# Down projection of the gated MLP: 16 of 22 feature blocks by Strassen's seven products, operand sums on GpSimd

## The chip, the core and the metric

One core of one Trainium2 chip runs the whole program in one launch. The metric is device time in microseconds (us); the median of three runs is compared. Engines are named as in the profile: PE (TensorE), ACT (ScalarE), DVE (VectorE), POOL (GpSimd), SP (SyncE, which here issues nearly all DMAs).

## What is computed

An encoder of two layers, batch 1, 1024 tokens, model width 1024, everything in float32. Layer 0 mixes tokens by latent attention and retention, layer 1 by gated linear attention. Each layer ends with the same MLP, and only its last product is touched here:

```python
def _conv_ffn(x, norm_g, w_up, conv_w, conv_b, w_down):
    h = _rmsnorm(x, norm_g)
    up = h @ w_up                                  # (1024, 1024) @ (1024, 2 * 2816)
    gate, val = up[..., :D_FF], up[..., D_FF:]
    gate = lax.conv_general_dilated(gate, ...) + conv_b    # depthwise, width 3
    return (jax.nn.silu(gate) * val) @ w_down      # (1024, 2816) @ (2816, 1024)
...
        x = x + _conv_ffn(x, ffn_norm[layer], ...)
```

## The kernel before

Activations lie transposed: features on the 128 partitions, tokens along the free dimension. A feature block is 128 features, a half is 512 tokens. The 2816 hidden features are 22 blocks (`NF`), the model width is 8 blocks (`NK`). Every float32 operand is held as two float32r parts, high and low, made by `split` (L327 on ACT writes the high part, L328 on DVE the low part), and every product is three matmuls (`mm3`, L349: high by high, high by low, low by high), each of one 128x128 weight block by 512 tokens.

**Up stage.** `up_fast` makes hidden block i (gate and value, both halves) by Strassen's algorithm in Winograd's form: seven products of four `mm3` instead of eight, with sums of weights on DVE (L1222 to L1225) and sums of activations kept in pages h1 to h4 (`T`). `gated_mid` applies the convolution and the gate; the result `cv` (128x1024) goes to DRAM (L1273, tile d).

**Down stage.** `down` computes the second product plainly. For each half of the tokens it holds all 22 hidden blocks as high and low parts (hx for the first 8, gh for the other 14), read back from d through the staging pages st (L1287). For each output block m it loads the weights in three pieces of 8, 8 and 6 hidden blocks (`wtile`, L340, pages raw), splits them (pages w), runs 66 matmuls into one PSUM bank, and adds the residual x (L1343). So a down stage has 2 x 8 x 66 = 1056 matmuls of 512 columns. In layer 0 the result is also normed for the next layer (`norm_add` L386 and L388, `norm_parts` L407); in layer 1 it is transposed (L1306) and written out.

**Order.** The tile framework puts each engine's instructions in an order of its own from the program's text, its dependences and its own estimates; each engine then runs its list strictly in that order, and waits on semaphores. SP's DMA issues are such a list too. A page of a pool is reused when its last reader is done.

Of the kernel before, what the change touches and what calls it, by code (L numbers as in the profile page):

```python
# [66 lines left out]
class Encoder:  # L67
# [1208 lines left out]
    def down(self, layer, mid, xs, gain=None, ahead=None):  # L1276

        nc, io = self.nc, self.io
        wdn = io["ffn_w_down"][layer].rearrange("(k p) f -> p k f", p=P)
        parts = [{}, {}]  # L1280

        def load(hf, ks):
            for k in ks:
                if k % 2 == 0:
                    two = self.page([P, 2, H2], tag="st")
                t = two[:, k % 2]
                nc.sync.dma_start(out=t, in_=mid[k][:, halves()[hf]])  # L1287
# [262 lines left out]
```

## Time and profile before

| | us |
|---|---|
| median of 3 runs | 2576.71 (2576.38 to 2578.4) |
| the profiled execution, its own time | 2580.83 |
| its span in the profile | 2579.0 |
| PE busy in the span | 2535.9 (98%) |
| DVE / ACT / POOL busy | 1649.4 / 1182.5 / 148.4 |
| mean granted PE clock | 0.998 |

The profiled execution took 4.1 us more than the median; 1.8 us of its time lie outside the span. Busy times of engines overlap, so they don't add up. Matmuls are pipelined: a matmul of 512 columns is shown with about 390 ns, but such matmuls follow one another at a shorter distance.

### The profile page before, as it was taken

Reading aid. Unit: us, or ns where it says so; the run is one execution under the profiler, and the core shown is the slowest. Engines: PE = TensorE matmul, PEld = TensorE weight load, DVE = VectorE, ACT = ScalarE, POOL = GpSimd, SP = SyncE. Lnnn points to the kernel's source line nnn. Section 1 sums busy time; section 2 is a strip of 40 time slices with the busy share of each in tenths; the row PEclk is TensorE's granted clock in tenths of the full one; section 3 lists DMA queues with packets and bytes.
Section 4 is the critical chain, followed back from the end, with each engine's and each line's share of the span. In section 5 each row is a group of like instructions: output and inputs, shape, how many; then the busy total and the mean of one; then the engine's idle time right before and its main releaser. Section 6 shows DMA issues by size and latency. Waiting matters only on the chain.

```text
span 2579.0 us, 33115 instructions
## 1 busy us (share of the span) xinstructions
PE 2535.9 (98%) x12776; PEld 2125.0 (82%) x12776; DVE 1649.4 (64%) x2607; ACT 1182.5 (46%) x2155; POOL 148.4 (6%) x222
## 2 busy tenths in 40 slices
PE   8999999999999999999999999999999999999999
PEld 8989877777888888887888898897788888887887
DVE  6545887878578677776363545648588776775331
ACT  5234767778444333344242445657443333334221
POOL 0000033443000000000000000000000000000000
PEclk9999999999999999999999999999999999999999
DMA  5111100003622222238443111223732222237443
GB/s 194 40 46 42 50 26 5 14 18 123 212 83 81 82 82 87 85 110 275 141 146 95 58 54 46 75 65 122 242 97 69 84 82 82 82 116 254 142 140 92
DMA packets 320596, 253.81 MB, mean 98 GB/s; under 512 B 14828, under 2 KB 271957, under 8 KB 320437
## 3 DMA queue, kind: packets, MB, share of 16 engines
q1 hardware_dynamic: 317877, 243.30, 30.2%
q0 software_dynamic: 2560, 8.39, 0.8%
q8 instruction: 100, 1.64, 0.3%
q14 instruction: 59, 0.48, 0.1%
HBM read 193.71 MB, written 57.93 MB: 98 GB/s over the span
## 4 chain that ended last, share of the span: by engine, by line
PE 84%; DVE 6%; ACT 5%; DMA 2%; issue 2%; SPq 0%; POOL 0%; DVEq 0%; ACTq 0%
PE mm L349 74%; PE mr L1102 1%; ACT w L327 1%; PE mr L349 1%; PE mr L1389 1%; PE mr L1444 1%; PE mr L1391 1%; DMA st<-d 1%; PE mr L852 1%; PE mr L1032 1%; DMA raw<-in_w_out_odd 1%; PE mr L1077 1%; DVE w L328 1%; DVE hx L328 1%; DVE sr L1445 1%
## 5 line engine op out<-in xcount | busy, mean ns | idle before, releaser
L349 PE MATMUL mm<-hx,w 128*128 128x512 f32 (+1 forms) x3600 | 867.7, 393 | 1.6 <-ACT hx L1241 1.4
L349 PEld LDWEIGHTS mm<-hx,w 128*128 128x128 f32 (+1 forms) x3600 | 670.6, 188 | 144.8 <-ACT hx L1241 2.2
L328 DVE TENSOR_TENSOR w<-raw,w 128x1024 fp32r<-128x1024 f32 (+2 forms) x271 | 297.1, 1098 | 301.3 <-ACT w L327 284.0
L327 ACT CAST w<-raw 128x1024 fp32r<-128x1024 f32 (+2 forms) x321 | 285.3, 893 | 415.6 <-PE mm L349 358.0
L349 PE MATMUL mm<-w,hx 128*128 128x256 f32 (+1 forms) x2304 | 364.4, 306 | 2.3 <-POOL w L328 1.7
L349 PE MATMUL mm<-h,wf 128*128 128x512 f32 x1368 | 328.9, 389 | 0.0
L349 PEld LDWEIGHTS mm<-w,hx 128*128 128x128 f32 x2304 | 308.1, 192 | 21.5 <-POOL w L328 2.7
L349 PE MATMUL mm<-gh,w 128*128 128x512 f32 x1344 | 314.7, 392 | 4.5 <-ACT gh L327 3.6
L349 PEld LDWEIGHTS mm<-h,wf 128*128 128x128 f32 x1368 | 256.8, 188 | 53.3
L349 PEld LDWEIGHTS mm<-gh,w 128*128 128x128 f32 x1344 | 250.2, 188 | 61.2 <-ACT gh L327 5.3
L1239 DVE TENSOR_TENSOR hx<-mm,hx 128x512 f32<-128x512 f32 x190 | 130.4, 687 | 154.1 <-PE mm L349 154.0
L327 ACT CAST wf<-raw 128x1024 fp32r<-128x1024 f32 x78 | 81.9, 1053 | 187.6 <-DVE raw L1225 118.1
L349 PE MATMUL mm<-hx,wf 128*128 128x512 f32 x552 | 131.9, 389 | 0.0
L349 PEld LDWEIGHTS mm<-hx,wf 128*128 128x128 f32 x552 | 103.6, 188 | 21.5
L349 PE MATMUL mm<-h,w 128*128 128x512 f32 x456 | 109.5, 389 | 0.0
L349 PE MATMUL mm<-hr,hr 128*128 128x512 f32 x336 | 104.1, 404 | 1.3 <-ACT hf L1473 1.3
L328 DVE TENSOR_TENSOR wf<-raw,wf 128x1024 fp32r<-128x1024 f32 x78 | 95.1, 1221 | 12.5 <-ACT wf L327 12.4
L349 PEld LDWEIGHTS mm<-h,w 128*128 128x128 f32 x456 | 85.6, 188 | 17.7
L1269 ACT ACTIVATE pg<-pg 128x1024 f32<-128x1024 f32 x44 | 46.7, 1062 | 107.1 <-DVE pg L1268 106.9
L1268 DVE SCALAR_TENSOR_TENSOR pg<-mm,c,pg 128x512 f32<-128x512 f32 (+1 forms) x100 | 74.0, 747 | 33.0 <-ACT pg L1263 32.9
L349 PE MATMUL mm<-hf,w 128*128 128x512 f32 x384 | 88.8, 392 | 0.0
L349 PEld LDWEIGHTS mm<-hf,w 128*128 128x128 f32 x384 | 72.2, 188 | 16.0
(364 smaller groups left out, 3057.3 us busy)
## 6 DMA issues: line engine op xcount, KB each, us to landing
raw<-in_ffn_w_up SPq DMA_DIRECT2D x88, 512.0 KB
raw<-in_ffn_w_down SPq DMA_DIRECT2D x64, 512.0 KB
st<-d SPq DMA_DIRECT2D x95, 256.0 KB
d<-pg SPq DMA_DIRECT2D x44, 512.0 KB
raw<-in_ffn_w_down SPq DMA_DIRECT2D x32, 384.0 KB
raw<-in_w_in_odd SPq DMA_DIRECT2D x24, 512.0 KB
raw<-in_w_out_even SPq DMA_DIRECT2D x16, 512.0 KB
raw<-in_w_out_odd SPq DMA_DIRECT2D x16, 512.0 KB
```

What stands on the lines that cost most here:

```text
L327: self.nc.scalar.copy(hi, src)
L328: return (rest or self.nc.vector).tensor_tensor(lo, src, hi.bitcast(F32), ALU.subtract)
L349: mm = lambda w, x, start, stop: self.nc.tensor.matmul(out, lhsT=w, rhs=x, start=start, stop=stop, skip_group_check=more)
L852: self.nc.tensor.transpose(ps[:, blk(j)], src[:, j], self.ident)
L1032: nc.tensor.matmul(ps[:, n], lhsT=k3[:, t % 4], rhs=vt(t), start=True, stop=True)
L1077: nc.tensor.matmul(p[:, blk(j)], lhsT=kc[:, blk(j)], rhs=qc[:, blk(j)], start=True, stop=True)
L1102: nc.tensor.matmul(ps, lhsT=w[:, blk(t % 4)], rhs=x, start=n == 0, stop=n == len(terms) - 1)
L1239: add = lambda out, x, y: nc.vector.tensor_tensor(out, x, y, ALU.add)
L1268: nc.vector.scalar_tensor_tensor(dst, g[hf][:, src], cw(tap), dst, ALU.mult, ALU.add)
L1269: nc.scalar.activation(cv, cv, AF.Silu)
L1389: nc.tensor.matmul(ps[:, :192], lhsT=e.cq[k][hf][:, blk(t % 4)], rhs=w1[:, k], start=k == 0, stop=k == 2)
L1391: nc.tensor.matmul(ps[:, 256:], lhsT=e.ckv[k][hf][:, blk(t % 4)], rhs=w2[:, k], start=k == 0, stop=k == 1)
```

## The change

Hidden blocks 0 to 15 go through Strassen's algorithm in the down projection, in two windows (w = 0 and 1) of eight blocks; blocks 16 to 21 stay plain.

- In a window, the even hidden blocks are the upper and the odd ones the lower half of the inner dimension, the two halves of the tokens are the two column blocks, and output blocks m and m + 1 are the two row blocks. A *visit* is one window and one pair of output blocks: seven products of four `mm3`, 84 matmuls, where the plain way takes 96. There are 8 visits in a layer (four pairs, two windows).
- The four sums of hidden blocks that Strassen needs are made in the up stage by POOL (`Mid.add`, four subtractions for each pair of blocks), and written to DRAM behind the next weight loads (`flush`). The tile d becomes seven operands for each window, 4 x 256 KB each.
- `operands` reads one operand of a window back (two loads of 512 KB through the pages pg and st) and splits it. Window 0's are read during the last steps of the up stage, into pages h1 to h4 and hx as these come free; window 1's during visit 3, each right behind the product that was the last to use its place. `rest` reads blocks 16 to 21 during visit 7.
- The weights of a visit are loaded once for both halves (four loads of 256 KB); their four sums are made by POOL (`weights`, `part`), and each of the seven is split by ACT and DVE six products ahead (`LEAD`).
- Each product is added by DVE into the residual or into a helper u (the first of window 0 copied by ACT); PSUM banks b1, b3 and b4 are used by two products of a visit, and the second accumulates on the first. After visits of window 1 POOL adds u to three results.
- The stores of the residual in `out_proj` are issued by ACT instead of POOL, and the program's scratch for software DMA is set to 4096.

```diff
+PAIRED, WIN, LEAD = 16, 8, 6
...
                 if hf:
                     for j in range(2):
-                        nc.gpsimd.dma_start(out=xs[2 * m + j], in_=self.xT[m][j])
+                        nc.scalar.dma_start(out=xs[2 * m + j], in_=self.xT[m][j])
...
-        mid = []
-        with self.room("left", h2=8), self.room("left", h3=8), self.room("left", h1=8), self.room("left", h4=8):
-            T = {n: [tuple(self.page([P, H2], F32R, f"h{n}") for _ in range(2)) for _ in range(4)] for n in range(1, 5)}
+        mid = Mid(self)
+        with ExitStack() as stack:
+            for n in (2, 3, 1, 4):
+                h4 = stack.enter_context(self.room("left", **{f"h{n}": 4}))
+            T = {n: self.pairs(f"h{n}") for n in range(1, 5)}
             self.xrooms.pop().close()
+            late = stack.enter_context(self.room("left", tt=4))
...
+            down = Down(self, layer, mid)
...
-                for g, then in zip(steps, steps[1:] + [None]):
+                for i, (g, then) in enumerate(zip(steps, steps[1:] + [None]), 3):
                     next(g)
                     if then:
                         next(then)
+                    else:
+                        for p in range(1, 5):
+                            down.operands(0, p)
+                        down.begin()
                     for _ in g:
                         pass
-        if gain is not None:
-            self.x_rooms()
-            with self.room("left", st=2), self.room("left", gh=28):
-                return self.down(layer, mid, xs, gain, ahead)
-        with self.room("left", st=2), self.room("left", gh=28), self.room("right", xt=8, yt=2):
-            self.down(layer, mid, xs)
+                    if i == PAIRED:
+                        mid.flush()
+                        late.close()
+                        late = stack.enter_context(self.room("left", st=1, wd=2))
+                    if i == NF - 2:
+                        down.operands(0, 0)
+                for p in range(5, 7):
+                    down.operands(0, p)
+            return down.run(xs, gain, ahead, stack, (late, h4))
+    def pairs(self, tag):
+        pages = [[self.page([P, 2, H2], F32R, tag) for _ in range(2)] for _ in range(2)]
+        return [tuple(x[:, j % 2] for x in pages[j // 2]) for j in range(4)]
...
+        mid.flush()
...
-        d = self.dp.tile([P, S], F32, name=self.nm("d"))
-        nc.sync.dma_start(out=d, in_=cv)
-        mid.append(d)
...
+        mid.add(i, cv)
...
+class Mid:
...
+        self.d = [[[e.waiting() for _ in range(2)] for _ in range(7)] for _ in range(PAIRED // WIN)]
+    def add(self, i, cv):
+        e, nc = self.e, self.e.nc
+        if i >= PAIRED:
+            d = e.dp.tile([P, 2, H2], F32, name=e.nm("d"))
+            nc.sync.dma_start(out=d.rearrange("p h f -> p (h f)"), in_=cv)
+            self.last.append(d)
+            return
+        w, j = divmod(i // 2, WIN // 2)
+        at = lambda p: self.d[w][p][j // 2][j % 2]
+        two = [cv[:, sl] for sl in halves()]
+        if i % 2 == 0:
+            self.first = two
+            nc.sync.dma_start(out=at(0), in_=two[0])
+            return
+        b11, b12, b21, b22 = *self.first, *two
+        nc.sync.dma_start(out=at(2), in_=b21)
+        nc.sync.dma_start(out=at(6), in_=b22)
+        t1, t2, t3, t4 = (e.page([P, H2], tag="tt") for _ in range(4))
+        for t, x, y in ((t1, b12, b11), (t2, b22, t1), (t3, b22, b12), (t4, b21, t2)):
+            nc.gpsimd.tensor_tensor(t, x, y, ALU.subtract)
+        self.late += [(at(p), t) for p, t in ((4, t1), (1, t2), (3, t3), (5, t4))]
+    def flush(self):
+        for d, t in self.late:
+            self.e.nc.sync.dma_start(out=d, in_=t)
+        self.late = []
...
+class Down:
...
+    A11, S2, A12, S3, S1, A22, S4 = range(7)
...
+    def operands(self, w, p):
+        e, nc, n = self.e, self.nc, {1: 2, 3: 3, 4: 1, 5: 4}.get(p)
+        out = e.pairs(f"h{n}") if n else [tuple(e.page([P, H2], F32R, "hx") for _ in range(2)) for _ in range(4)]
+        self.b[w][p] = out
+        for a, d in enumerate(self.mid.d[w][p]):
+            self.n = getattr(self, "n", -1) + 1
+            two = e.page([P, 2, H2], tag="st" if self.n % 4 == 3 else "pg")
+            nc.sync.dma_start(out=two, in_=d.rearrange("j p f -> p j f"))
+            if n:
+                e.split(two, *(bass.AP(x.tensor, x.offset, [list(x.ap[0]), [H2, 2], [1, H2]]) for x in out[2 * a]))
+            else:
+                for j in range(2):
+                    e.split(two[:, j], *out[2 * a + j])
+    def weights(self, v):
+        e, nc, (w, m) = self.e, self.nc, self.visits[v]
+        wg, wv = (e.page([P, 2, WIN // 2, P], F32, "raw") for _ in range(2))
+        for x, c in ((wg, m), (wv, m + 1)):
+            src = self.w[:, blk(w, WIN), blk(c)].rearrange("p (j two) f -> p two j f", two=2)
+            for i in range(2):
+                nc.sync.dma_start(out=x[:, i], in_=src[:, i])
+        s1, s4 = (e.page([P, WIN // 2, P], tag="hx") for _ in range(2))
+        nc.gpsimd.tensor_tensor(s1, wv[:, 0], wv[:, 1], ALU.add)
+        nc.gpsimd.tensor_tensor(wv[:, 0], wg[:, 0], wv[:, 0], ALU.subtract)
+        self.raw[v] = {self.A11: wg[:, 0], self.S2: wg[:, 0], self.A12: wg[:, 1], self.S3: wv[:, 0], self.S1: s1,
+                       self.A22: wv[:, 1], self.S4: s4}
+    def part(self, s):
+        if s >= 7 * len(self.visits):
+            return
+        e, nc, (v, p) = self.e, self.nc, divmod(s, 7)
+        if not p:
+            self.weights(v)
+        r = self.raw[v]
+        t = e.page([P, 2, WIN // 2, P], F32R, "wd" if p in (self.S1, self.A22) else "w")
+        e.split(r[p], t[:, 0], t[:, 1])
+        self.parts[s] = t
+        if p == self.A11:
+            nc.gpsimd.tensor_tensor(r[p], r[self.S1], r[p], ALU.subtract)
+        if p == self.A12:
+            nc.gpsimd.tensor_tensor(r[self.S4], r[p], r[self.S2], ALU.subtract)
+    def begin(self):
+        for s in range(LEAD):
+            self.part(s)
+    def product(self, s, ps, first):
+        t, b = self.parts.pop(s), self.b[self.visits[s // 7][0]][s % 7]
+        for j in range(WIN // 2):
+            self.e.mm3(ps, (t[:, 0, j], t[:, 1, j]), b[j], first and j == 0, j == WIN // 2 - 1, not first)
+    def visit(self, v):
+        e, nc, (w, m) = self.e, self.nc, self.visits[v]
+        last = m == NK - 2
+        for i in range(2):
+            for hf in range(2):
+                if not w:
+                    nc.sync.dma_start(out=self.x[m + i][hf], in_=self.xs[2 * (m + i) + hf])
+        (c11, c12), (c21, c22) = self.x[m], self.x[m + 1]
+        if not w:
+            self.u[m] = e.page([P, H2], tag="hx")
+        u = self.u[m]
+        b1, b2, b3, b4 = (e.bank() for _ in range(4))
+        for p, (ps, outs) in enumerate(((b1, [u]), (b2, [u]), (b1, [c11]), (b3, [c22]), (b4, [c22]), (b3, [c21]), (b4, [c12]))):
+            s = 7 * v + p
+            self.product(s, ps, p in (0, 1, 3, 4))
+            for x in outs:
+                if not w and p == 0:
+                    nc.scalar.copy(x, ps)
+                else:
+                    nc.vector.tensor_tensor(x, ps, x, ALU.add)
+            self.part(s + LEAD)
+            if last and not w:
+                self.operands(1, p)
+            if last and w and p in (1, 3, 4):
+                self.rest({1: 0, 3: 2, 4: 4}[p], {1: 2, 3: 3, 4: 1}[p])
+        if w:
+            for x in (c21, c12, c22):
+                nc.gpsimd.tensor_tensor(x, x, u, ALU.add)
+    def rest(self, k, n):
+        e = self.e
+        for k in (k, k + 1):
+            two = e.page([P, 2, H2], tag="st" if k % 4 == 3 else "pg")
+            self.nc.sync.dma_start(out=two, in_=self.mid.last[k])
+            parts = [e.page([P, 2, H2], F32R, f"h{n}") for _ in range(2)]
+            e.split(two, *parts)
+            self.b[1][7 + k] = parts
...
+    def run(self, xs, gain, ahead, stack, ends):
+        e, nc, io = self.e, self.nc, self.e.io
+        self.xs, self.u = xs, {}
+        if gain is not None:
+            e.act_set(LN_EXP)
+            e.x_rooms()
+            e.new_x()
+            self.x = e.xT
+        else:
+            stack.enter_context(e.room("right", xt=2 * NK))
+            self.x = [[e.page([P, H2], tag="xt") for _ in range(2)] for _ in range(NK)]
+        for v in range(len(self.visits)):
+            self.visit(v)
+        if gain is None:
+            for room in ends:
+                room.close()
+            stack.enter_context(e.room("left", yt=2))
...
+        for hf in range(2):
+            for m in range(NK):
+                wh, wl = e.wtile(self.w[:, PAIRED:, blk(m)], [P, NF - PAIRED, P])
+                ps, x = e.bank(), self.x[m][hf]
+                for k in range(NF - PAIRED):
+                    b = [t[:, hf] for t in self.b[1][7 + k]]
+                    e.mm3(ps, (wh[:, k], wl[:, k]), b, k == 0, k == NF - PAIRED - 1)
...
+    nc = bacc.Bacc("TRN2", target_bir_lowering=False, num_devices=1, dynamic_dma_scratch_size=4096)
```

How instructions stand, at three places.

**ACT, start of layer 0's down stage.** Before: the casts of step 21's gate (pg) and of the hidden blocks (st) follow one another, and nothing that PE needs for a used PSUM bank stands among them.

```order
L1263 ACTIVATE pg_10743<-hx_10612,c_70 128x512
L327 CAST hx_10796<-st_10794 128x512
L327 CAST hx_10801<-st_10794 128x512
L1269 ACTIVATE pg_10743<-pg_10743 128x1024
L327 CAST hx_10807<-st_10805 128x512
L327 CAST hx_10812<-st_10805 128x512
L327 CAST gh_10818<-st_10816 128x512
L327 CAST gh_10823<-st_10816 128x512
L327 CAST w_10980<-raw_10978 128x1024
```

Now: from the gate of step 21 (pg_10956) through the casts of operands 5 (h) and 6 (hx) to the copy of the first product of visit 0, which is the last row.

```order
L1281 ACTIVATE pg_10956<-hx_10719,c_70 128x512
L328 CAST h_10968<-pg_10972 128x1024
L328 CAST h_10970<-st_10976 128x1024
L1287 ACTIVATE pg_10956<-pg_10956 128x1024
L328 CAST hx_10980<-pg_10988 128x512
L328 CAST hx_10982<-pg_10988 128x512
L328 CAST hx_10984<-pg_10994 128x512
L328 CAST hx_10986<-pg_10994 128x512
L145 ACT_TABLE_LOAD
L1415 COPY hx_11028<-mm_11029 128x512
```

The copy that clears bank mm_11029 for its second product stands behind both casts of operand 6's second load and an activation table load.

**DVE, middle of the down stage.** Before: output blocks 5 and 6 of the first half; between two evictions (L1343) stand three low parts of weights and one sum of squares.

```order
L1343 TENSOR_TENSOR xb_10904<-mm_11355,xb_10904 128x512
L328 TENSOR_TENSOR w_11552<-raw_11549,w_11551 128x768
L388 TENSOR_TENSOR pg_11082<-pg_11082 128x512
L328 TENSOR_TENSOR w_11581<-raw_11578,w_11580 128x1024
L328 TENSOR_TENSOR w_11611<-raw_11608,w_11610 128x1024
L1343 TENSOR_TENSOR xb_10906<-mm_11488,xb_10906 128x512
L328 TENSOR_TENSOR w_11641<-raw_11638,w_11640 128x768
L388 TENSOR_TENSOR pg_11082<-pg_11082 128x512
```

Now: visit 3, while window 1's operands come in (h and hx are operands, mm_11428 to mm_11431 are the visit's four banks b1 to b4, w are weights).

```order
L329 TENSOR_TENSOR h_11498<-pg_11503,h_11497 128x1024
L1417 TENSOR_TENSOR xb_11020<-mm_11428,xb_11020 128x512
L329 TENSOR_TENSOR w_11520<-raw_11481,w_11520 128x512
L329 TENSOR_TENSOR hx_11524<-pg_11531,hx_11523 128x512
L1417 TENSOR_TENSOR xa_11023<-mm_11430,xa_11023 128x512
L329 TENSOR_TENSOR hx_11526<-pg_11531,hx_11525 128x512
L329 TENSOR_TENSOR w_11556<-raw_11481,w_11556 128x512
L329 TENSOR_TENSOR hx_11528<-st_11537,hx_11527 128x512
L329 TENSOR_TENSOR h_11561<-pg_11564,h_11560 128x1024
L329 TENSOR_TENSOR hx_11530<-st_11537,hx_11529 128x512
L329 TENSOR_TENSOR h_11563<-pg_11568,h_11562 128x1024
L1417 TENSOR_TENSOR xa_11023<-mm_11431,xa_11023 128x512
```

Between the evictions of bank b3 (mm_11430) and bank b4 (mm_11431) stand six low parts, five of them of operands; all six are first needed in the next visit.

## Rows read from the trace of the kernel before

**Rows 1.** Page, part 1: busy us of each engine, share of the span, instructions.

```profile
PE 2535.9 (98%) x12776; PEld 2125.0 (82%) x12776; DVE 1649.4 (64%) x2607; ACT 1182.5 (46%) x2155; POOL 148.4 (6%) x222
```

**Rows 2.** Windows: from:to, length, busy us by engine, PEclk, DMA share, GB/s.

```profile
830.00:1143.00 313.00, 313.00 (x1383) 259.26 (x1382) 228.63 (x317) 110.57 (x132) 0.00 (x0) 1.00 0.26 83
1180.00:1200.00 20.00, 19.14 (x81) 14.58 (x81) 12.12 (x17) 10.83 (x17) 0.00 (x0) 1.00 0.91 288
1200.00:1410.00 210.00, 210.00 (x929) 173.92 (x928) 93.25 (x117) 70.90 (x95) 0.00 (x0) 1.00 0.49 150
2360.00:2574.00 214.00, 213.62 (x971) 176.56 (x969) 67.16 (x75) 56.84 (x74) 0.00 (x0) 1.00 0.46 138
```

**Rows 3.** Timeline, PE: start us, us, engine, line, operation, count.

```profile
1165.81 11.04 PE L349 MATMUL mm<-hx,w 128*128 128x512 f32 x48
...
1394.79 5.60 PE L349 MATMUL mm<-hx,w 128*128 128x512 f32 x24
...
1409.75 5.60 PE L349 MATMUL mm<-hx,w 128*128 128x512 f32 x24
...
2322.76 11.06 PE L349 MATMUL mm<-hx,w 128*128 128x512 f32 x48
...
2563.81 9.81 PE L349 MATMUL mm<-gh,w 128*128 128x512 f32 x42
```

**Rows 4.** Chain that ended last, longest pieces: start us, us, what.

```profile
1174.96 4.48 DMA st<-d
...
2339.29 5.33 DMA st<-d
...
2378.73 15.02 PE mm L349 x66
2394.18 15.00 PE mm L349 x66
```

**Rows 5.** Timeline, layer 1: a weight load issued, and the waiting cast.

```profile
2359.94 1.25 SPq L340 DMA_DIRECT2D raw<-in_ffn_w_down  x2
...
2364.26 1.06 ACT L327 CAST w<-raw 128x1024 fp32r<-128x1024 f32 x1 [3.56 <-DMA raw<-in_ffn_w_down]
```

**Rows 6.** Groups by line, DVE, 1166 to 1410 us: count, busy, mean ns.

```profile
L328 DVE TENSOR_TENSOR w<-raw,w 128x1024 fp32r<-128x1024 f32 x30 | 36.7, 1225 | 85.9 <-ACT w L327 85.6 <-DMA st<-d 0.3
L328 DVE TENSOR_TENSOR gh<-st,gh 128x512 fp32r<-128x512 f32 x28 | 18.5, 690 | 12.1 <-ACT gh L327 12.0
L328 DVE TENSOR_TENSOR w<-raw,w 128x768 fp32r<-128x768 f32 x16 | 15.3, 955 | 0.7 <-PE mm L349 0.6
L407 DVE SCALAR_TENSOR_TENSOR pg<-xb,c,pg 128x512 f32<-128x512 f32 x8 | 5.7, 748 | 0.1
L1343 DVE TENSOR_TENSOR xa<-mm,xa 128x512 f32<-128x512 f32 x8 | 5.5, 691 | 11.7 <-PE mm L349 11.7
```

**Rows 7.** Groups by line, ACT, same stretch.

```profile
L327 ACT CAST w<-raw 128x1024 fp32r<-128x1024 f32 x31 | 32.6, 1051 | 87.8 <-PE mm L349 80.2 <-issue 4.4 <-DMA raw<-in_ffn_w_down 3.2
L327 ACT CAST gh<-st 128x512 fp32r<-128x512 f32 x28 | 17.1, 621 | 16.3 <-DMA st<-d 15.7
```

**Rows 8.** Groups by line, POOL, whole span.

```profile
L328 POOL TENSOR_TENSOR w<-raw,w 128x512 fp32r<-128x512 f32 x48 | 63.8, 1329 | 125.8 <-ACT w L327 82.6 <-issue 15.5 <-PE mm L349 13.0
```

**Rows 9.** One line (L1501): count, shortest/median/longest ns.

```profile
L1501 DVE SCALAR_TENSOR_TENSOR pg<-pg,pg x8: 685/1623/1725, 441.1 to 656.4; 128x512 f32<-128x512 f32 x8
```

**Rows 10.** Timeline of DVE and POOL around one of those eight.

```profile
514.98 1.29 POOL L328 TENSOR_TENSOR w<-raw,w 128x512 fp32r<-128x512 f32 x1 [2.56 <-PE mm L349]
515.15 1.67 DVE L1501 SCALAR_TENSOR_TENSOR pg<-pg,pg 128x512 f32<-128x512 f32 x1
```

**Rows 11.** Timeline of DVE, one step of the up projection.

```profile
1098.47 1.29 DVE L1271 TENSOR_TENSOR pg<-pg,hx 128x512 f32<-128x512 f32 x2
...
1103.45 0.69 DVE L1239 TENSOR_TENSOR hx<-mm,hx 128x512 f32<-128x512 f32 x1 [0.55 <-PE mm L349]
...
1108.88 0.69 DVE L1239 TENSOR_TENSOR hx<-mm,hx 128x512 f32<-128x512 f32 x1 [3.61 <-PE mm L349]
```

More of the change, by code (lines that the diff above doesn't have):

```diff
@@ L1271, in gated_mid @@
             nc.vector.tensor_tensor(cv[:, sl], cv[:, sl], v[hf], ALU.mult)
-        d = self.dp.tile([P, S], F32, name=self.nm("d"))
-        nc.sync.dma_start(out=d, in_=cv)
-        mid.append(d)
[L1276 to L1287, printed above, removed]
-                parts[hf][k] = [self.page([P, H2], F32R, "hx" if k < 8 else "gh") for _ in range(2)]
-                self.split(t, *parts[hf][k])
-        def norm(hf):
-            self.norm_parts(out, hf, gain, self.norm_scale(self.bank(), D))
-        load(0, range(NF))
-        if gain is not None:
-            self.act_set(LN_EXP)
-            self.new_x()
-        wait = []
+        mid.add(i, cv)
@@ new lines, with __init__ @@
+class Mid:
+    def __init__(self, e):
+        self.e, self.last, self.late = e, [], []
+        self.d = [[[e.waiting() for _ in range(2)] for _ in range(7)] for _ in range(PAIRED // WIN)]
[24 more added lines that the diff above has]
+        self.late = []
@@ new lines, with __init__ @@
+class Down:
+    A11, S2, A12, S3, S1, A22, S4 = range(7)
+    def __init__(self, e, layer, mid):
+        self.e, self.nc, self.mid = e, e.nc, mid
+        self.w = e.io["ffn_w_down"][layer].rearrange("(k p) f -> p k f", p=P)
+        self.visits = [(w, m) for w in range(PAIRED // WIN) for m in range(0, NK, 2)]
+        self.b, self.parts, self.raw = [{}, {}], {}, {}
+    def operands(self, w, p):
[97 more added lines that the diff above has]
+            stack.enter_context(e.room("left", yt=2))
+        wait, done = [], []
+        def norm(hf):
+            e.norm_parts(out, hf, gain, e.norm_scale(e.bank(), D))
@@ L1300, in write @@
         def write(x, hf, m):
             if m % 4 == 0:
-                wait.append(self.page([P, 4, H2], tag="yt"))
-            ps = self.bank()
+                wait.append(e.page([P, 4, H2], tag="yt"))
+            ps = e.bank()
             for t in range(4):
-                nc.tensor.transpose(ps[:, blk(t)], x[:, blk(t)], self.ident)
+                nc.tensor.transpose(ps[:, blk(t)], x[:, blk(t)], e.ident)
             nc.scalar.copy(wait[0][:, :, blk(m % 4)], ps.rearrange("p (t f) -> p t f", f=P))
@@ L1314, in write @@
                 wait.pop()
[L1316 to L1323 removed]
+        for hf in range(2):
[5 more added lines that the diff above has]
+                    e.mm3(ps, (wh[:, k], wl[:, k]), b, k == 0, k == NF - PAIRED - 1)
                 while done:
                     write(*done.pop(0))
[L1326 to L1342 removed]
                 nc.vector.tensor_tensor(x, ps, x, ALU.add)
                 if gain is not None:
[L1345 removed]
+                    e.norm_add(x, m)
                     if hf and m == LAG[0]:
[L1347 removed]
+                        out = e.new_split(NK, "hx")
                         norm(0)
@@ L1537 @@
     from concourse.bass_utils import run_bass_kernel_spmd
-    nc = bacc.Bacc("TRN2", target_bir_lowering=False, num_devices=1)
+    nc = bacc.Bacc("TRN2", target_bir_lowering=False, num_devices=1, dynamic_dma_scratch_size=4096)
     arrays, io = {}, {}
```

25 lines of the change are left out of this document (removed).

## The prediction

> **What bounds the kernel now.** I read the page first: PE is busy 2535.9 us of a span of 2579.0, DVE 64%, ACT 46%, POOL 6% [rows 1]. So matmuls count, and I went on by stage. In the up stage PE is busy 313 of 313 us, in the down stages 210 of 210 and 213.6 of 214, once the first 30 us are over; there DVE is at 44% and less, while in the up stage it is at 73% [rows 2]. The granted clock is 1.00 in each of these windows, so neither stage has anything to gain or lose from it as long as PE goes on without a gap.
>
> How far apart do matmuls follow? The timeline of PE shows it better than a matmul's own 390 ns: from 1394.79 to 1409.75 us there are the 24 + 42 matmuls of one output block [rows 3], so one takes 14.96 / 66 = 0.2267 us, and a Strassen product of 12 takes 2.72.
>
> That gives what a down stage loses. Layer 0's runs from 1165.81 to 1409.75, 243.9 us, for 1056 matmuls, 239.4 us: 4.6 us lost. Layer 1's runs from 2322.76 to the last 42 matmuls at 2563.81, 241.05 us, for 1014 matmuls (229.9) and 15 groups of transposes, each 15.45 - 14.96 = 0.49 us by the distance of two blocks [rows 3, 4]: 3.9 us lost. All 8.4 us go in the first 30 us of a stage, where the chain of waits shows loads of the hidden blocks, 4.48 to 5.33 us each [rows 4], at 288 GB/s with the DMA engines 0.91 busy [rows 2]. That is the nearest this trace has to a ceiling of DMA.
>
> **The change, term by term.**
>
> *Matmuls.* Before, 22 x 8 x 2 x 3 = 1056 in a layer. Now 8 visits x 7 products x 4 x 3 = 672, and 6 x 8 x 2 x 3 = 288 for blocks 16 to 21: 960. The 96 fewer are 21.8 us a layer, **-43.5 us** in all. PE has no other work in these stages, so every microsecond counts, if no new gap opens.
>
> *A plain visit* (19.0 us of PE). DVE has seven evictions (0.69 us each) and seven low parts of weights (0.69), 9.7 us; ACT seven casts of 0.62 us; POOL four weight sums of 1.33 us, and in window 1 three more additions, 9.3 us [rows 6 to 8]. Weights are split six products, 16 us, ahead, and their load is 1 MB for 19 us. Nothing here reaches 19 us: 0. The narrow place is a bank's second product: only one product (2.72 us) lies between the two, and the eviction has to fit into it.
>
> *Start of the stage.* Seven operands (14 loads of 524 KB, 7.3 MB), the weights of two visits (2.1 MB), four residual blocks (1.0) and a store (0.5) make 11 MB, 38 us at 288 GB/s. In the program's list they begin ahead of the last step but one's store, some eight products or 22 us before the stage, and the last is needed seven products, 19 us, into it: 41 us. That is tight, as it was before. At its end stands ACT's list: the copy that frees the first bank is behind the casts of operand 6, whose second load waits for a staging page. I take the 4.2 us a layer that the old start lost, **0** net. Below, 1 us a layer (only the last cast and low part exposed); above, 8 (one more round of a load, a cast and a low part).
>
> *Switch to window 1, in visit 3.* This is new. DVE gets 14 operand pages on top of the visit: 8 low parts of 1024 columns (1.225 us), 12 of 512 (0.69), 7 of weights, 7 evictions, together 27.7 us [rows 6] in 19.0 us of PE. The surplus, 8.7 us, can go on into visit 4, but DVE works in order. Follow the third place shown from the program, with the visit's start as 0. Operand 1 may take its place when product 2 ends, at 5.4. After a cast (1.05 us [rows 7]) DVE has a low part of 1.225, two of 0.69, an eviction, and h_11498's own 1.225: that one ends at 11.0 and frees its staging page. The next load into the page takes 4.3 us (issued at 2359.94, used at 2364.26 [rows 5]) to 6.2 (5.33 us [rows 4] for 256 KB, and 0.9 for another 256 KB at 288 GB/s); with the cast and the low part h_11563 that makes 17.6 to 19.5. DVE's own list from h_11498 to the eviction of bank b4, eleven instructions, takes 9 x 0.69 + 2 x 1.225 = 8.7 us. So the bank is clear at 19.7 to 20.2. PE wants it at 17.7 (six products and six matmuls of visit 4 stand ahead of it): 2.0 to 2.5 us lost. At visit 4's third product the same steps give 0.2 to 1.4 us more, behind the last operands. So 2.2 to 3.9 a layer; I take 3, **+6 us**. Ends: 0, and 8.7 a layer if all surplus falls on PE.
>
> *Blocks 16 to 21, and the end of layer 0.* A block is now 18 matmuls, 4.1 us, instead of 66. In the last eight blocks (32.6 us) DVE has an eviction, a sum and a weight tile each (0.69 + 0.69 + 0.955), the normalisation of the first half (8 x (0.748 + 0.69)) and the next stage's first weights (1.225): 31.4 us [rows 6]. The normalisation can't begin until the first half's sum has gone through PE, ACT and DVE, which leaves DVE some 3.5 us idle; so it ends 2 to 3 us after PE, and the next stage waits. Before, this lay under 8 x 15 us. **+2.5 us**, between 0 and 5, once (layer 1 has no such norm).
>
> *End of the kernel.* The last store but one, 768 KB, is now issued 4.6 us ahead of the last instead of 15.45; it needs 2.7 us at 288 GB/s. **+0.5 us**, 0 to 1.
>
> *Up stage.* POOL gets four subtractions for each pair of blocks, 16 pairs in both layers, about 1.33 us each [rows 8], 5.3 us of the 38 us of two steps. POOL itself is idle there. But a DVE instruction that normally takes 0.685 us took 1.725 elsewhere in this kernel [rows 9], and the timeline shows why: POOL began a subtraction at 514.98 and ended at 516.27; the DVE instruction, with two inputs in SBUF as POOL's, began at 515.15 and ended at 516.82, which is 0.55 after POOL [rows 10]. So each POOL instruction can hold DVE by 1.04 us. Behind the two multiplications that feed POOL, DVE has four such instructions, then 0.55 us of idle time and, 4 us later, 3.61 us more [rows 11]. Four holds are 4.2 us; they fit into these 4.16 us. I take 0; the other end is 4.2 us a pair, 67 us.
>
> The Trainium skill (page "SBUF — State Buffer", section "Who interferes with whom") states that a DVE instruction with two SBUF inputs contends with a GpSimd instruction that reads SBUF, under an exclusive lock: whichever begins first keeps it to its end. The trace agrees (0.685 against 1.67 us in the timeline). By that rule alone, without the idle time, the sum below would be 67 us higher.
>
> *Residual stores on ACT.* 16 issues a layer on an engine that is 46% busy [rows 1], their data ready: 0. Two issues of SP take 1.25 us [rows 5]; if nothing covered them, 10 us a layer.
>
> Sum: -43.5 + 0 + 6 + 2.5 + 0.5 = **-34.5 us** on the profiled execution's 2580.8, 2546.3. That execution stood 4.1 us above the median, so 2542 as a median.
>
> **Rivals.** (A) As summed, transitions half hidden: 2535 to 2550, chance 0.60. (B) Transfers and DVE bound the transitions: starts at 8 us, switches at 8.7, 5 at the layer's end and 1 at the last store, +31.4 us: 2564, in a band from 2550 to 2568. For it: 0.91 DMA share already [rows 2], and 7.3 MB in 19 us at the switch would be 386 GB/s, so that only early loading and late use save it; against it: four staging pages filled ahead. 0.20. (C) The up stage pays for POOL: holds delay an eviction that PE waits for. At 4.2 us for each of 16 pairs 67 us come back: 2609, slower than before. It decides from 34.5 / 16 = 2.2 us a pair on. For it: [rows 9, 10] and DVE at 73%. Against it: the idle 3.61 us, and that up-stage banks b3 and b4 have two products between their uses. 0.09. (D) The change gives all that it says and the early loads hide the starts too: -43.5 - 8.4 = 2525, up to 2534. For it: operands begin 22 us ahead of the stage. 0.11. That the matmuls don't fall isn't open: PE's list is 192 shorter in 512-column matmuls.
>
> **Numbers.** The time is A's, 2542. 2528 to 2562 holds A, half of D and about two thirds of B, 0.8. About 0.2% (5 us) is what a measurement of this kernel can tell from no change. Faster: A, D, 0.18 of B, 0.01 of C, 0.90; same 0.04; slower 0.06, all of it C.
>
> **What would show it.** Right: down stages some 20 us shorter, PE without a gap within visits 0 to 2 and 5 to 7; gaps of 2 to 5 us at the start, 1 to 4 around visits 3 and 4, with DVE's evictions (L1417) as releaser; up steps still seven products, 19.0 us, long. Wrong if the up steps of odd blocks grow, with POOL ahead of DVE (C), if loads into pg and st release PE for over 8 us a layer (B), or if a plain visit takes longer than 19.2 us, since its one-product slack for evictions is then too small.

## Result and profile after

The changed kernel takes 2608.28 us (median of 4 runs, 2604.34 to 2611.61), the kernel before beside it 2577.03 (2576.38 to 2578.4): a ratio of 1.012, 95% interval 1.0102 to 1.0138. It is slower by 31 us. The forecast was 2542, 2528 to 2562. The profiled execution of after took 2607.8 us with a span of 2605.7, 26.7 longer than the span of before; the two profiles are compared below on that.

Page of after, part 1 (answers to [rows 1]):

```profile
PE 2511.6 (96%) x12584; PEld 2091.0 (80%) x12584; DVE 1811.3 (70%) x2763; ACT 1202.1 (46%) x2215; POOL 370.4 (14%) x342
```

192 matmuls fewer, as the change says, and yet PE is busy only 24.3 us less in a longer span. So PE waits, where before it hardly did, and some of its matmuls run at a lower clock (below). Where it waits, the windows by stage show. First the up stage of layer 0 and of layer 1 in after, each from the first fast step's copy of bank b1 to the last one's (columns as in [rows 2]):

```profile
804.53:1158.97 354.44, 342.93 (x1489) 278.15 (x1490) 270.83 (x340) 118.91 (x145) 45.71 (x28) 1.00 0.31 99
1972.94:2334.71 361.77, 346.06 (x1489) 280.41 (x1490) 270.93 (x340) 118.95 (x144) 45.62 (x28) 0.99 0.30 98
```

The same stretches in before:

```profile
805.97:1144.25 338.28, 337.64 (x1489) 279.67 (x1490) 244.84 (x336) 119.75 (x144) 0.00 (x0) 1.00 0.26 84
1962.93:2301.20 338.27, 337.63 (x1489) 279.67 (x1490) 244.85 (x336) 119.71 (x143) 0.00 (x0) 1.00 0.26 84
```

The matmuls are the same number (1489), the stage is 16.2 and 23.5 us longer, and DVE is busy 26 us more in each with four instructions more. Instructions that were there already take longer. The groups by line of after, 830 to 1130 us (count, busy us, mean ns, then the idle time before them and its releaser), name them:

```profile
L329 DVE TENSOR_TENSOR w<-sw,w 128x512 fp32r<-128x512 f32 x15 | 24.5, 1634 | 0.0
L1243 DVE TENSOR_TENSOR raw<-raw 128x512 f32<-128x512 f32 x15 | 17.2, 1147 | 0.5
L1242 DVE TENSOR_TENSOR raw<-sw,raw 128x512 f32<-128x512 f32 x15 | 13.6, 908 | 0.0
L1257 DVE TENSOR_TENSOR hx<-mm,hx 128x512 f32<-128x512 f32 x75 | 51.2, 683 | 1.4 <-PE mm L350 1.4
L329 DVE TENSOR_TENSOR w<-raw,w 128x1024 fp32r<-128x1024 f32 x15 | 18.4, 1225 | 46.4 <-ACT w L328 46.4
L328 ACT CAST w<-raw 128x1024 fp32r<-128x1024 f32 x15 | 15.7, 1050 | 52.0 <-DMA raw<-in_ffn_w_up 52.0
L1321 POOL TENSOR_TENSOR tt<-pg,tt 128x512 f32<-128x512 f32 x14 | 22.8, 1630 | 135.1 <-DVE pg L1289 135.1
```

The first three of them in before, same stretch:

```profile
L328 DVE TENSOR_TENSOR w<-sw,w 128x512 fp32r<-128x512 f32 x16 | 10.9, 683 | 0.0
L1225 DVE TENSOR_TENSOR raw<-raw 128x512 f32<-128x512 f32 x16 | 11.1, 692 | 0.6
L1224 DVE TENSOR_TENSOR raw<-sw,raw 128x512 f32<-128x512 f32 x16 | 10.9, 680 | 0.0
```

Three DVE instructions with both inputs in SBUF take 1634, 1147 and 908 ns on average; they took 683, 692 and 680 in before. The evictions (L1257), with one input in PSUM, stay at 683. And ACT now waits 52 us for weights, 3.5 us in a step. A step is 19.04 us long in before, the distance of two copies of b1. In after, layer 0, from the third step on, those with one subtraction take 19.4 to 19.6 us, those with three 20.8 to 21.0. When no subtraction is left, one more step takes 19.9 (its weights came late, see the end) and the last three 18.2 to 18.6, as the delay is worked off.

How the delay goes round, the timeline of after shows, around an odd block's three subtractions and on to the next step's sums:

```profile
996.67 1.52 POOL L1321 TENSOR_TENSOR tt<-pg,tt 128x512 f32<-128x512 f32 x1 [18.02 <-DVE pg L1289]
996.96 1.78 DVE L329 TENSOR_TENSOR w<-sw,w 128x512 fp32r<-128x512 f32 x1
998.15 1.74 POOL L1321 TENSOR_TENSOR tt<-pg,pg 128x512 f32<-128x512 f32 x1
998.66 0.68 DVE L1257 TENSOR_TENSOR hx<-mm,hx 128x512 f32<-128x512 f32 x1
999.26 1.17 DVE L1242 TENSOR_TENSOR raw<-sw,raw 128x512 f32<-128x512 f32 x1
999.85 1.74 POOL L1321 TENSOR_TENSOR tt<-pg,tt 128x512 f32<-128x512 f32 x1
1000.47 1.66 DVE L1243 TENSOR_TENSOR raw<-raw 128x512 f32<-128x512 f32 x1
...
1003.25 1.23 DVE L329 TENSOR_TENSOR wf<-raw,wf 128x1024 fp32r<-128x1024 f32 x1 [0.51 <-ACT wf L328]
...
1004.50 2.12 SPq L1229 DMA_DIRECT2D raw<-in_ffn_w_up  x2
...
1008.18 1.05 ACT L328 CAST w<-raw 128x1024 fp32r<-128x1024 f32 x1 [3.54 <-DMA raw<-in_ffn_w_up]
1009.27 1.23 DVE L329 TENSOR_TENSOR w<-raw,w 128x1024 fp32r<-128x1024 f32 x1 [3.06 <-ACT w L328]
1010.41 0.68 DVE L1257 TENSOR_TENSOR hx<-mm,hx 128x512 f32<-128x512 f32 x1
1011.13 0.82 ACT L1281 ACTIVATE pg<-hx,c 128x512 f32<-128x512 f32 x1 [1.89 <-DVE hx L1257]
...
1017.78 1.78 DVE L329 TENSOR_TENSOR w<-sw,w 128x512 fp32r<-128x512 f32 x1
```

Read it as a loop. The sums of weights (L1240 to L1243) end late by the holds; so the cast and the low part wf do; they free the raw page, and the next weights are issued only then (1004.50). They can be used 3.68 us later (1008.18). DVE stands idle for 3.06 us meanwhile, then makes the low part of w, the eviction, the convolution, and comes to the next sums late. Here lies the idle time on which the prediction built: 3.61 us before [rows 11], 3.06 now. What ends it is no longer PE, but the cast that waits for the transfer.

In a pair of steps the DVE instructions are held 1.78 - 0.68, 1.17 - 0.68, 1.66 - 0.68 and 1.78 - 0.68 = 3.7 us in all, and the pair takes 19.4 + 20.8 = 40.2 us instead of 38.1: 2.1 us lost.

In the down stage the timeline of PE in after, layer 0, shows the gaps (visit 0 begins at 1186.60; a product is 2.72 us):

```profile
1179.40 4.60 PE L350 MATMUL mm<-h,wf 128*128 128x512 f32 x12 [4.15 <-DVE hx L1257]
...
1203.19 4.58 PE L350 MATMUL mm<-h,wd 128*128 128x512 f32 x12 [2.83 <-DVE xa L1417]
...
1225.61 3.06 PE L350 MATMUL mm<-h,wd 128*128 128x512 f32 x12 [1.48 <-DVE xa L1417]
...
1265.90 3.01 PE L350 MATMUL mm<-h,wd 128*128 128x512 f32 x12 [1.88 <-DVE xa L1417]
...
1292.64 7.29 PE L350 MATMUL mm<-hx,w 128*128 128x512 f32 x24 [2.82 <-ACT wd L328]
```

The sixth product (weights wd, bank b3 for the second time) waits for the eviction of the fourth in visits 0, 1 and 3. From 1299.77 on there is no gap in visits 5 to 7.

Behind the longest of these gaps the product itself is slow: at 1179.40, 1203.19 and 1292.64, and at 2354.23 and 2377.46 in layer 1, its 12 matmuls need 4.1 to 4.5 us instead of 2.72. A window shows why (columns as in [rows 2]):

```profile
1180.20:1183.60 3.40, 3.40 (x10) 2.66 (x9) 3.40 (x7) 2.57 (x5) 0.00 (x0) 0.50 0.74 246
```

The granted clock is 0.50 there, the lower level of 1.2 GHz; so it is at the other four places, after PE had stood idle for 2.3 to 4.2 us. Together this costs 8.2 us; in the down stages of before the clock stayed at 1.00.

### The profile page after: what moved, and what is told of

It reads as the page before. It is cut to its first block, busy times and chain, and to the rows that moved or that the text cites. A ratio compares the mean times of both kernels' runs of the same rounds, so it can differ in the third digit from the quotient of the medians.

```text
span 2605.7 us, 33289 instructions
## 1 busy us (share of the span) xinstructions
PE 2511.6 (96%) x12584; PEld 2091.0 (80%) x12584; DVE 1811.3 (70%) x2763; ACT 1202.1 (46%) x2215; POOL 370.4 (14%) x342
## 3 DMA queue, kind: packets, MB, share of 16 engines
q8 instruction: 99, 1.62, 0.3%
## 5 line engine op out<-in xcount | busy, mean ns | idle before, releaser
L350 PE MATMUL mm<-hx,w 128*128 128x512 f32 (+1 forms) x3408 | 828.2, 394 | 11.1 <-ACT wd L328 4.4
L350 PEld LDWEIGHTS mm<-hx,w 128*128 128x128 f32 (+1 forms) x3408 | 635.3, 188 | 150.2 <-ACT hx L1259 3.6
L328 ACT CAST w<-raw 128x512 fp32r<-128x512 f32 (+2 forms) x321 | 255.6, 807 | 449.7 <-PE mm L350 217.6
L329 DVE TENSOR_TENSOR w<-raw,w 128x1024 fp32r<-128x1024 f32 (+2 forms) x271 | 268.1, 994 | 260.8 <-ACT w L328 245.2
L350 PE MATMUL mm<-h,w 128*128 128x512 f32 x1416 | 336.6, 390 | 0.0
L350 PEld LDWEIGHTS mm<-w,hx 128*128 128x128 f32 x2304 | 307.7, 192 | 21.5 <-POOL w L329 2.9
L350 PEld LDWEIGHTS mm<-h,w 128*128 128x128 f32 x1416 | 264.7, 188 | 54.7
L1321 POOL TENSOR_TENSOR tt<-pg 128x512 f32<-128x512 f32 x16 | 28.2, 1761 | 958.9 <-DVE pg L1289 734.9
L1257 DVE TENSOR_TENSOR hx<-mm,hx 128x512 f32<-128x512 f32 x190 | 129.8, 683 | 13.3 <-PE mm L350 13.3
L350 PE MATMUL mm<-h,wd 128*128 128x512 f32 x384 | 95.0, 401 | 12.1 <-DVE xa L1417 6.2
L350 PEld LDWEIGHTS mm<-h,wd 128*128 128x128 f32 x384 | 73.5, 193 | 30.3 <-issue 8.9
L1321 POOL TENSOR_TENSOR tt<-pg,tt 128x512 f32<-128x512 f32 x32 | 52.2, 1632 | 293.2 <-DVE pg L1289 293.2
```

What stands on the lines that cost most here:

```text
L328: self.nc.scalar.copy(hi, src)
L329: return (rest or self.nc.vector).tensor_tensor(lo, src, hi.bitcast(F32), ALU.subtract)
L350: mm = lambda w, x, start, stop: self.nc.tensor.matmul(out, lhsT=w, rhs=x, start=start, stop=stop, skip_group_check=more)
L1257: add = lambda out, x, y: nc.vector.tensor_tensor(out, x, y, ALU.add)
L1321: nc.gpsimd.tensor_tensor(t, x, y, ALU.subtract)
```

## Experiments

**Is it the subtractions, or the stores and SyncE's longer queue?** Three kernels ran for this. The first takes the subtractions out and keeps the stores:

```diff
-        t1, t2, t3, t4 = (e.page([P, H2], tag="tt") for _ in range(4))
-        for t, x, y in ((t1, b12, b11), (t2, b22, t1), (t3, b22, b12), (t4, b21, t2)):
-            nc.gpsimd.tensor_tensor(t, x, y, ALU.subtract)
+        if i == 1:
+            self.fixed = [e.page([P, H2], tag="tt") for _ in range(4)]
+            for t in self.fixed:
+                nc.gpsimd.memset(t, 0.5)
+        t1, t2, t3, t4 = self.fixed
```

> The change with the four GpSimd subtractions of each pair left out: four tiles filled once are stored in their place, as many bytes at the same places (operands S1 to S4 of the down stage are constants, so that part of the product is not computed). Theory A (the subtractions hold VectorE's two-input instructions, and the up stage's loop from operand sums over weight transfer back to the next sums has under 1 us of slack a step): a pair of steps falls from 40.2 us to 38.1 us, the stage from 354 and 362 us to about 338 us each, time 2608 - 39 = 2569 us (2562 to 2576). Theory B (the 64 stores and SyncE's longer queue make the next weights late): no change, 2602 to 2612 us.

Measured: 2565.86 us (2564.07 to 2566.48), 0.9953 of before (0.9938 to 0.9968). From the third on, all steps are 19.04 us, and both up stages take 338.25, as in before. So the subtractions are worth the 42 us between the two kernels.

The second keeps the subtractions and takes the stores out:

```diff
-        self.late += [(at(p), t) for p, t in ((4, t1), (1, t2), (3, t3), (5, t4))]
...
-        for a, d in enumerate(self.mid.d[w][p]):
+        for a, d in enumerate(self.mid.d[w][{1: 2, 3: 0, 4: 6, 5: 0}.get(p, p)]):
```

> The change with the four subtractions kept, and the 4 stores of their results a pair left out; the down stage reads stored pieces in their place (S1 to S4 are not the right sums, so that part is not computed). Theory A: the up stage stays at 354 and 362 us, time 2604 to 2610 us. Theory B: steps fall back towards 19.04 us, time 2569 to 2585 us.

Measured: 2612.37 us (2609.09 to 2614.74), 1.0134 (1.0119 to 1.0149); stages of 353.2 and 359.6 us. That is 2.4 us above theory A's range; the stores cost nothing that shows, and theory B falls.

The third puts the subtractions alone into the kernel before:

```diff
...
         mid.append(d)
+        two = [cv[:, sl] for sl in halves()]
+        if i >= 16:
+            return
+        if i % 2 == 0:
+            self.even = two
+            return
+        b11, b12, b21, b22 = *self.even, *two
+        t1, t2, t3, t4 = (self.page([P, H2], tag="tt") for _ in range(4))
+        for t, x, y in ((t1, b12, b11), (t2, b22, t1), (t3, b22, b12), (t4, b21, t2)):
+            nc.gpsimd.tensor_tensor(t, x, y, ALU.subtract)
...
```

(The lines left out make room for four pages tt and set the scratch for software DMA to 4096, as in after.)

> The kernel before with nothing added but the four GpSimd subtractions a pair for the first 16 blocks, whose results are not used; no stores, no other down stage. Theory A: steps of 19.4 and 20.8 us in turn instead of 19.04, 14 to 16 pairs in both layers at 2.1 to 2.4 us: 2577 + 35 = 2612 us (2605 to 2618), with VectorE's 128x512 subtraction beside GpSimd at 1.2 to 1.8 us instead of 0.68. Theory B: 2577 us, within 4.

Measured: 2614.93 us (2610.28 to 2616.34), 1.0142 (1.0126 to 1.0157). Results that nobody reads cost 37 us: steps of 19.4 to 19.7 and 20.8 to 21.1 us in turn in layer 0, stages of 353.4 and 356.0 us, together 32.9 longer than in before. The timeline of this kernel shows the same holds as that of after:

```profile
996.75 1.58 POOL L1284 TENSOR_TENSOR tt<-pg,tt 128x512 f32<-128x512 f32 x1 [17.92 <-DVE pg L1271]
997.10 1.78 DVE L328 TENSOR_TENSOR w<-sw,w 128x512 fp32r<-128x512 f32 x1
998.29 1.73 POOL L1284 TENSOR_TENSOR tt<-pg,pg 128x512 f32<-128x512 f32 x1
999.41 1.17 DVE L1224 TENSOR_TENSOR raw<-sw,raw 128x512 f32<-128x512 f32 x1
```

**What in a subtraction holds DVE?** Each is replaced by a memset of the same tile, which writes as much and reads nothing:

```diff
-            nc.gpsimd.tensor_tensor(t, x, y, ALU.subtract)
+            nc.gpsimd.memset(t, 0.5)
```

> The change with each of the four GpSimd subtractions of a pair replaced by a GpSimd memset of the same tile, which reads nothing (S1 to S4 are constants, so that part is not computed); the waits on it and the stores of its result stay. Theory R (only a GpSimd instruction that reads SBUF holds VectorE's two-input instructions): steps of 19.04 us, VectorE's subtractions 0.68 us throughout, 2608 - 42 = 2566 us (2560 to 2572). Rival (any GpSimd instruction beside VectorE holds it, or the stores at their later place cost): 2585 to 2612 us.

Measured: 2573.47 us (2565.88 to 2577.5), 0.9985 (0.9975 to 0.9994), 1.5 above the range given; both up stages take 338.25 us. But this is not the test that it was meant to be. A memset reads nothing, so it waits for nothing in the up stage, and the framework moved all 64 of them ahead: they run at 623 to 712 and 1803 to 1885 us, and no GpSimd instruction is left in the up stage's steps. Their length says no more than that of the kernel without subtractions. What decides is where the memsets do run beside DVE, in the timeline of this kernel:

```profile
621.88 1.35 POOL L329 TENSOR_TENSOR w<-hf,w 128x512 fp32r<-128x512 f32 x1 [1.55 <-ACT w L328]
622.84 0.95 DVE L329 TENSOR_TENSOR hx<-hr,hx 128x512 fp32r<-128x512 f32 x1 [0.76 <-ACT hx L328]
623.18 1.92 POOL L1321 MEMSET tt<- 128x512 f32 x4
623.71 0.68 DVE L329 TENSOR_TENSOR w<-hf,w 128x512 fp32r<-128x512 f32 x1
624.31 1.28 DVE L329 TENSOR_TENSOR hx<-hr,hx 128x512 fp32r<-128x512 f32 x2
```

The first low part on DVE begins beside a GpSimd instruction that reads SBUF, ends 0.56 us after it, and takes 0.95 us. The next three, with two inputs in SBUF too, run beside memsets and take the usual time. So do all 25 low parts of this kernel that meet a memset and no reading GpSimd instruction: 12 of 512 columns at 677 to 693 ns, 13 of 1024 at 1217 to 1228. So what holds DVE is that GpSimd reads SBUF, not that it is at work. The Trainium skill says so (page "SBUF — State Buffer", section "Who interferes with whom": a two-input DVE instruction contends with a GpSimd instruction that reads SBUF, not with one that only writes it); these rows agree, and so does the eviction at 998.66 in after, which has one input in PSUM and takes 0.68 us in the midst of a GpSimd subtraction. A memset is also shorter (0.53 us) than a subtraction.

**Why does a hold cost PE anything, with DVE idle for 4 us a step?** A third page for raw weights lets the first of a step's two loads go out before the last step's sums are done; the subtractions stay:

```diff
-            with self.room("right", wf=6, sw=2):
+            with self.room("right", wf=6, sw=2, ry=1):
...
-        wg, wv = (self.page([P, NK, P], F32, "raw") for _ in range(2))
+        wg, wv = (self.page([P, NK, P], F32, "ry" if n % 3 == 2 else "raw") for n in (2 * i, 2 * i + 1))
```

> The change as it is, GpSimd's subtractions with it, and a third page for the raw weights of the up stage in place of two, so that the first of a step's two weight loads needn't wait for the operand sums of the step before. Theory A (the hold costs because the loop operand sums, low part, page free, weight transfer, low part of w, eviction, sums has little slack): the wait of ScalarE for the weights, 120 us in all in the changed kernel, goes, and steps come back to 19.04 us with the hold still there (subtractions of 1.2 to 1.8 us on VectorE): 2608 - 36 = 2572 us (2564 to 2585). Rival (VectorE has no time for the hold wherever it falls): 2600 to 2612 us.

Measured: 2575.15 us (2569.21 to 2580.51), 0.9989 (0.998 to 0.9999), 33 us less than the changed kernel. From the fifth of the 18 steps on, all are 19.04 us. ACT's wait for these weights falls from 120.1 us to 3.8 (DVE's sums wait 39.5 us for weights instead, the second load of a step among them). The holds are still there, at another place: groups by line, 830 to 1130 us:

```profile
L329 DVE TENSOR_TENSOR w<-raw,w 128x1024 fp32r<-128x1024 f32 x11 | 22.2, 2014 | 0.0
L1321 POOL TENSOR_TENSOR tt<-pg,pg 128x512 f32<-128x512 f32 x7 | 15.9, 2275 | 0.0
L1243 DVE TENSOR_TENSOR raw<-raw 128x512 f32<-128x512 f32 x12 | 12.2, 1014 | 0.3
```

The low part of w takes 2014 ns instead of 1225, and PE doesn't feel it. The holds sum to some 22 us in this stretch, where after has 24.5. The hold alone is not the cost; it costs because of the loop through the two raw pages.

**How much does the loop bear?** Two of the four subtractions stay, one in each step:

```diff
...
-        for t, x, y in ((t1, b12, b11), (t2, b22, t1), (t3, b22, b12), (t4, b21, t2)):
...
+        t2, t4 = self.fixed
+        t1, t3 = (e.page([P, H2], tag="tu") for _ in range(2))
+        for t, x, y in ((t1, b12, b11), (t3, b22, b12)):
```

> The change with two of the four GpSimd subtractions of a pair left, one beside each of its two steps (t1 in the even block's step, t3 in the odd one's); the other two operands are constants stored in their place (S2 and S4 are not computed). Each step then holds VectorE by about 1.1 us (one subtraction of 1.78 instead of 0.68 us). Theory A with slack: the changed kernel's steps with one such hold took 19.4 us, so 0.4 us of the 1.1 is lost a step, 0.7 us a pair: 2566 (without any) + 15 x 0.7 = 2577 us (2570 to 2583). Rival without slack (each us of hold is a us of PE): 2.2 us a pair, 2566 + 33 = 2599 us (2592 to 2606).

Measured: 2579.26 us (2576.62 to 2582.44), 1.0002 (0.9992 to 1.0011). From the fifth on, steps of layer 0 are 19.2 to 19.55 us while subtractions run; w<-sw takes 1574 ns on average (+0.9), and no other DVE instruction is held. So about 0.4 of 0.9 us is lost; the loop bears some 0.5 us a step. In layer 1 four steps are longer (20.2 to 21.5 us); their weights came late, as at the end of this text.

**The same sums on DVE.** One word is changed:

```diff
-            nc.gpsimd.tensor_tensor(t, x, y, ALU.subtract)
+            nc.vector.tensor_tensor(t, x, y, ALU.subtract)
```

> The change with the four subtractions of a pair made by VectorE instead of GpSimd. Four of about 0.68 us are 2.7 us a pair on VectorE in place of a hold of 3.7 us. Theory A: the loop absorbs about 1.5 us a pair (3.7 held, 2.2 lost), so 1.2 us a pair stays: 2608 - 16 x 1.0 = 2592 us (2584 to 2600). Theory B: no change, 2602 to 2612 us.

Measured: 2566.41 us (2562.15 to 2569.66), 0.9959 (0.9945 to 0.9973). Faster than both theories allowed, and as fast as with no sums at all. Late steps of layer 0 are 19.04 us. My price took the order on DVE as fixed, and it wasn't. The timeline of this kernel, after an odd block's three sums:

```profile
1027.35 3.84 SPq L1229 DMA_DIRECT2D raw<-in_ffn_w_up  x2
...
1031.15 1.05 ACT L328 CAST w<-raw 128x1024 fp32r<-128x1024 f32 x1 [1.64 <-DMA raw<-in_ffn_w_up]
1031.41 0.69 DVE L1257 TENSOR_TENSOR hx<-mm,hx 128x512 f32<-128x512 f32 x1 [0.64 <-PE mm L350]
1032.14 0.82 ACT L1281 ACTIVATE pg<-hx,c 128x512 f32<-128x512 f32 x1
1032.24 1.23 DVE L329 TENSOR_TENSOR w<-raw,w 128x1024 fp32r<-128x1024 f32 x1
```

The eviction that feeds the gate now stands ahead of the low part of w (in after, 1009.27 and 1010.41, behind it), so that the gate no longer waits for the weights. The framework, which orders by its own estimates, moved it when DVE's list grew; with the sums on GpSimd the order stayed what it is without them. That this order is what made the sums free is argued from these rows; no run separates it.

**The rest of GpSimd's work.** In that kernel, the weight sums of the down stage and the additions of u go to DVE too:

```diff
-        nc.gpsimd.tensor_tensor(s1, wv[:, 0], wv[:, 1], ALU.add)
-        nc.gpsimd.tensor_tensor(wv[:, 0], wg[:, 0], wv[:, 0], ALU.subtract)
+        nc.vector.tensor_tensor(s1, wv[:, 0], wv[:, 1], ALU.add)
+        nc.vector.tensor_tensor(wv[:, 0], wg[:, 0], wv[:, 0], ALU.subtract)
...
-                nc.gpsimd.tensor_tensor(x, x, u, ALU.add)
+                nc.vector.tensor_tensor(x, x, u, ALU.add)
```

> The kernel of e4_dve_sums with GpSimd's work of the down stage (four weight sums a visit of two output blocks, three additions of u a visit of the second window) given to VectorE too, so that GpSimd computes nothing in either stage. Theory L (the gaps of 1 to 2 us behind VectorE's evictions in the plain visits come from the same hold): the gaps of the second to fourth visit, 4.1 us in layer 0 and 5.1 us in layer 1, fall under 1 us each, and something of the start: 2566 - 8 = 2558 us (2550 to 2563). Theory D (VectorE is late there from its own queue, which the sums make longer by 2.7 us a visit): gaps as long or longer, 2564 to 2580 us.

Measured: 2549.28 us (2547.63 to 2553.55), 0.989 of before (0.9873 to 0.9906): faster than the kernel before by 28 us, and than the kernel with only the first sums moved by 17. That is 0.7 us below the range of theory L. Two groups by line, 1190 to 1260 us, with the sums on GpSimd:

```profile
L329 DVE TENSOR_TENSOR h<-pg,h 128x1024 fp32r<-128x1024 f32 x7 | 9.6, 1372 | 0.2 <-ACT h L328 0.2
L329 DVE TENSOR_TENSOR hx<-pg,hx 128x512 fp32r<-128x512 f32 x6 | 5.4, 920 | 2.5 <-ACT hx L328 2.5
```

and the same two with all sums on DVE:

```profile
L329 DVE TENSOR_TENSOR h<-pg,h 128x1024 fp32r<-128x1024 f32 x7 | 8.5, 1219 | 0.3 <-ACT h L328 0.3
L329 DVE TENSOR_TENSOR hx<-pg,hx 128x512 fp32r<-128x512 f32 x4 | 2.7, 686 | 2.5 <-ACT hx L328 2.5
```

What PE loses in visit 1 (1.2 and 2.4 us in the two layers of the kernel before this one) falls to 0.4 and 0, around visits 3 and 4 from 7.2 and 7.7 to 2.8 and 1.7. A weight sum also takes GpSimd 1.35 to 1.48 us on average and DVE 0.69, so the weights are ready sooner; hold and length were not told apart here.

## Why the prediction was wrong, by its own steps

Losses of PE below are distances of products in the timeline, less 0.2267 us a matmul, layer 0 first.

- **Up stage, 0: this step failed.** It cost 16.2 + 23.5 = 39.7 us. The hold itself was sized well: 1.04 us each from [rows 9, 10], 1.1 measured, 3.7 us for a pair where 4.2 was the bound. Wrong was that they "fit into these 4.16" us of idle time. The sign named for rival C came: steps of odd blocks grew, with POOL ahead of DVE. Idle time of DVE at one place is not slack when it lies beside a transfer that DVE itself released. In before, 3.61 us of it [rows 11] ran beside the weight load; move DVE's sums later, and the load ends later by as much. The slack was that of the loop, and the trace of before could have told it, in its timeline of a step:

```profile
1029.14 6.07 SPq L1212 DMA_DIRECT2D raw<-in_ffn_w_up  x2
...
1033.46 1.05 ACT L327 CAST w<-raw 128x1024 fp32r<-128x1024 f32 x1
```

  From issue to cast are 4.32 us, and after shows that the weights can be used 3.68 us after their issue; so 0.64 us between landing and use (an estimate from two kernels), close to the 0.5 that the run with two subtractions gave. Rival C had the right place, and a size of 4.2 us a pair where 2.1 to 2.3 came in layer 0, and more in layer 1. Its ground against, the idle 3.61 us, is the one that fell. That its 2609 us is within 1 us of the measured median is luck: the up stages cost 27 us less than it said, and the down stages lost 22 us more than the sum that it was added to.
- **Matmuls, -43.5: right.** 192 fewer, and PE's windows without gaps.
- **Start of the stage, 0: mis-sized.** Losses of 10.8 and 9.1 us against 4.6 and 3.9 before: +11.4, beyond the upper end of 8 a layer. The releaser is DVE's list (evictions L1257 and L1417), not a load as the term had it. With no GpSimd work 7.6 and 10.5 are left, mostly behind DVE's low parts.
- **Plain visits, 0: mis-sized.** Visit 1 lost 1.8 and 2.1 us, at the "narrow place" that the text named and priced at nothing: with DVE held, an eviction doesn't fit into the one product. Visit 2 and, from the second product of visit 5 on, visits 5 to 7 do run without a gap in layer 0.
- **Switch, +6: mis-sized.** 8.7 and 6.9 us, 15.6 in all. Without GpSimd's sums 4.5: the chain of low parts that was followed step by step had no hold in it.
- **The clock, no term.** The text says that nothing is lost to it "as long as PE goes on without a gap", forecasts gaps of 2 to 5 us, and gives them no price beyond their length. 8.2 of the 31 us of the last three points are matmuls at a granted clock of 0.50 behind such gaps.
- **End of layer 0, +2.5, and tail, +0.5:** 0.3 and 0.7.

Sum: -43.5 + 39.7 + 11.4 + 3.9 + 15.6 + 1.0 = +28.1; the first up stage also begins 1.4 us earlier, which makes +26.7, as the spans differ. For the kernel with all sums on DVE the same list gives -43.5 + 1.8 (up stages) + 9.6 + 0.4 + 4.5 = -27.2, and its span is 27.2 us shorter. (Rival B's +31.4 comes to 31.0 by its own terms; nothing hangs on it.) So without GpSimd's sums the change was worth 27 of the 34.5 us that were forecast; the choice of the engine for its sums took them away.

## What to carry to other kernels

An engine's idle time takes up added work only if nothing that the engine released runs beside it: follow the loop (page freed, transfer, use, page freed again), and take what it is shorter than PE's step as the slack (here some 0.6 us of 19); one more page was worth 33 us here, with the same holds. Before work is given to GpSimd because it is idle, look at what DVE does at that time: a GpSimd instruction that reads SBUF, 1.5 to 1.8 us long, held DVE's two-input ones by 0.5 to 1.1 us each, and DVE did the same work in 0.68.
